# Triangular inverses of a gated delta net: 3 stream transpositions on 128 partitions per set in place of 12 on 32

## The chip, the cores and the metric

The kernel runs on one core of a Trainium2 chip. The metric is device time in microseconds (us), the median of several runs of the whole program.

## What is computed

Two layers of a diffusion backbone over 1024 latent and 256 context tokens with 1024 features. Layer 0 mixes tokens by latent attention and gated linear attention, layer 1 by a bidirectional chunked gated delta net with 8 heads; each is followed by a squared-ReLU MLP. The change touches the delta net alone. For each head, direction and chunk of 64 tokens it solves a unit lower triangular system:

```python
    a_mat = jnp.where(strict, jnp.einsum('bhnid,bhnjd->bhnij', kb, k) * decay, 0.0) + jnp.eye(C, dtype=F32)
    rhs = jnp.concatenate([v * beta, kb * jnp.exp(g)[..., None]], axis=-1)
    sol = lax.linalg.triangular_solve(a_mat, rhs, left_side=True, lower=True)
```

The kernel forms the inverse of each 64x64 matrix from its two 32x32 diagonal blocks and the product that fills the corner.

## The kernel before

TensorE runs the dense projections of layer 1 in program order: `dense1` takes a chunk of 128 output features at a time, in blocks of 512 or 256 tokens; a block of 512 is 24 matmuls (three products of split operands times eight slices of the features, lines 181 to 183) into one of four PSUM tiles `ps`. Queries and keys come first, then eight chunks of values, then the output gates. For queries, keys and values the block is emptied by ScalarE (L1146) and by two VectorE additions of the short convolution (L1151); for the gates by one SiLU on ScalarE (L1449).

All other work of this stage is in generators, called lanes. After each block, `pump` lets every lane go on by a share of the block's time, so that its instructions are written between the dense ones; each engine then runs what it has in that order. `drain` writes out what is left in the lanes once five gates have been projected. Three gates follow the drain, and then the scans of the delta net.

`inv_lane` makes the inverses in five sets, in the order 0, 1, 4, 2, 3: sets 0 to 3 are the latent chunks of a pair of heads, set 4 the context chunks of all pairs. A set is 32 matrices of 64x64 (two directions, 16 chunks) for each of the two heads of a pair; the head and the row lie on the partitions, so that each quarter of 32 partitions holds the rows of one 32x32 diagonal block. A set goes as follows.

- Products of keys, TensorE `pk` (L1349); VectorE multiplies them into `Nm` and, but for set 4, query-key products into `Am` (L1352).
- Four VectorE stream transpositions, one per quarter, bring the diagonal blocks of `Nm` into `X` (L1365).
- The loop: 30 steps of two VectorE operations on all 128 partitions (L1371 and L1373), the forward substitution of all blocks at once.
- GpSimd masks `X` (L1376) and sets its diagonal (L1377).
- Eight stream transpositions, two per quarter: one into `W` (L1386), one into `Y` (L1387). GpSimd copies a part of `W` into `Y` and clears the corner of `Y` (L1389, L1390).
- `inv_tail`, two pumps later: TensorE makes `pq` from `Nm` and `W` (L1403), ScalarE copies it to `Q` (L1407); in the next pump TensorE makes `pu` from `Q` and `W` (L1417), ScalarE copies it into the corner of `Y` (L1420), and GpSimd scales and stores `Y`.

`decay_lane` prepares the decays of the sets ahead. It has two buffers for `Nm`, and starts on a set when `state["inv"]` of the set two before it has been marked. GpSimd also makes the low parts of the weights (`wlo`, L170), ScalarE their high parts (`whi`, L167).

Of the kernel before, what the change touches and what calls it, by code (L numbers as in the profile page):

```python
# [8 lines left out]
F32 = mybir.dt.float32  # L9
# [12 lines left out]
T = LAT + CTX  # L22
# [11 lines left out]
def hybrid_backbone(ctx: ExitStack, tc: tile.TileContext, a, out, taps=None):  # L34
# [25 lines left out]
    def pump(us):  # L60
        """advances every lane: a lane yields the vector engine's time of what it emitted, or None to wait for the next call."""
        for it in list(lanes):
            gen, w = it
            t = us * w
            while t > 0:
                try:
                    d = next(gen)
                except StopIteration:
                    lanes.remove(it)
                    break  # L70
                if d is None:
                    break
                t -= d
# [39 lines left out]
    def ada_lane(l, mods, cols, wpool, accpool, ppool, ptag, wait=1):  # L113
        """modulations of layer l: products on the vector engine, sums over the partitions on the tensor engine."""
# [25 lines left out]
    def ada_first(m, half, wpool, ypool, ppool):  # L140
        """half of a modulation of layer 0 before there is other work: products on the tensor engine, then transposed."""
# [43 lines left out]
    def group(ps, n, nk, w, x, rate, every=1e9):  # L185
        """ps = sum over k of w(k)^T x(k), split operands; the lanes advance by rate of its time."""
# [12 lines left out]
    def rsqrt_small(p, ssq, n, dim, gain=1.0):  # L199
        """ssq: AP [128, n] (sums); returns tile [128, n] with gain/sqrt(mean + eps): a seed from the exponent, a step of  # L200
        third and one of second order."""
# [16 lines left out]
    def rsqrt_pool(p, ssq, n, dim):  # L218
        """as rsqrt_small, on the pool engine."""
# [13 lines left out]
    def stat_lane(hs, c0, n, tp, small, pp, ptag, dim, inc=False, engs=(V, G)):  # L233
        """1/rms of the tokens c0..c0+n over the features in the tiles hs, [128 tokens, n/128]; inc: as the tiles are made."""
# [22 lines left out]
    def spread(r, nt, pp, ptag):  # L257
        """r [128 tokens, nt] along the free dimension, the same on every partition: PSUM [128, nt * 128]."""
# [10 lines left out]
    def norm_lane(hs, c0, n, A, B, dst, tp, small, pp, ptag, r=None, inc=False, rb=None, ks=range(KD)):  # L269
        """a = rms(h) * A + B of a block of tokens, split into dst(k)."""  # L270
# [21 lines left out]
    class Act:  # L292
        """split activations [features, tokens] in tiles of one block of tokens."""
# [13 lines left out]
    # =========================================================== layer 0 mixer  # L307
# [23 lines left out]
    def gla_gates(g):  # L331
        """per head: decays of both directions (partitions 0..63 forward, 64..127 backward), decayed queries and keys."""
# [62 lines left out]
    def gla_main(g):  # L395
        """per head: states before every chunk, outputs, norm over the head, gate; transposed into d_mix."""
        f_order = list(range(16, 20)) + list(range(16))
        b_order = list(range(19, 15, -1)) + list(range(15, -1, -1))
        for h in range(4):
# [4 lines left out]
            # a chunk's outer product goes to the slot of the state after it  # L404
# [109 lines left out]
    with ExitStack() as e1:  # L514
# [146 lines left out]
        def latent(j, i, hs):  # L661
            """a chunk of the query (j = 0) or key-value (j = 1) latents, with its part of the sums of squares."""
# [26 lines left out]
    # ---- multi-head latent attention: scores transposed, minus the queries' maxima in a row of the contraction  # L689
# [7 lines left out]
    def proj(m, nm, kt, xh, xl, w, pp, tag):  # L697
        """generator of the projected blocks."""
# [8 lines left out]
    with ExitStack() as e2:  # L707
# [26 lines left out]
        # values  # L734
# [12 lines left out]
        # rotated query parts, scaled  # L747
# [54 lines left out]
    def prep0(k, b, eng):  # L802
        """a chunk of the heads' outputs, split for the output projection."""
# [5 lines left out]
    with ExitStack() as e2:  # L809
# [8 lines left out]
        def pair_ops(m):  # L818
            """projections of the heads 2m, 2m + 1 into their slots, a block of tokens at a time."""
# [24 lines left out]
        def max_ops(hd, b):  # L844
            """the row maxima of the scores of a block of queries into the contraction's last row: subtracted as rounded to
            the leading part, which the softmax does not depend on."""
# [91 lines left out]
    # =========================================================== output projection, residual; MLP  # L938
# [7 lines left out]
    def out_proj(l, wname, passes, mix, prep, base, act, add, stack, wp, w, span, sp=None):  # L946
        """h = base + gate * (mix @ w) in passes over blocks of tokens; prep[b]: what makes the blocks of pass b."""
# [42 lines left out]
    def mlp(l, blocks, tail_blocks, act, lanes_in, tail, wp, then=None):  # L990
        """h += gate * mlp(act); lanes_in(pools) makes the blocks after the first, tail(pools, b) follows a finished block."""
# [105 lines left out]
    # =========================================================== layer 1 mixer: gated delta rule  # L1097
    # A chunk of a head pair sits on the partitions as (head of the pair, token of the chunk or key feature).
    d_h = dram.tile([KD, 128, T], F32, name="d_h")
    d_X = [dram.tile([128, NC, 3, 64], F32, name=f"d_X{m}") for m in range(4)]          # keys transposed, keys, queries transposed  # L1100
# [9 lines left out]
    with ExitStack() as e1:  # L1110
# [12 lines left out]
        with ExitStack() as e2:  # L1123
# [16 lines left out]
            # ---- short convolution over tokens, SiLU  # L1140
# [25 lines left out]
            def qk_lane(y, nt, gain, m, key):  # L1166
                """a pair of conv'd heads: rows of length gain, to DRAM as they are (keys) and transposed."""
# [46 lines left out]
            # ---- gates  # L1214
# [22 lines left out]
            gx, gy = iv.tile([128, 2, 4, NC], F32, name="gx", tag="Q", bufs=2), iv.tile([128, 2, 4, NC], F32, name="gy", tag="tm")  # L1237
# [37 lines left out]
            # ---- decays, triangular inverses and masked query-key products of 32 chunks, both directions  # L1275
# [12 lines left out]
            def decay_lane():  # L1288
                """exp(-|g_i - g_j|) of a set; m < 4: the latent chunks of pair m, m == 4: the context chunks of all pairs."""
# [528 lines left out]
```

## Time and profile before

| | us |
|---|---|
| median of 3 runs (3552.53 to 3554.66) | 3552.6 |
| span of the profiled execution, first to last instruction | 3550.4 |
| TensorE busy in the span | 3322.8 (94%) |
| VectorE busy | 2329.7 (66%) |
| ScalarE busy | 1156.1 (33%) |
| GpSimd busy | 1077.5 (30%) |
| the inversions, from the first set's products to the last set's `pu` | 2106 to 2478 |

The profile gives one time for the profiled execution, its span; the 2.2 us to the median lie around it. PE is TensorE, DVE is VectorE, ACT is ScalarE, POOL is GpSimd. Busy time of an engine is the time in which an instruction of its own runs; matmuls are pipelined, so their recorded durations overlap. A wait is put down to the instruction whose end came last.

### The profile page before, as it was taken

Reading aid. Unit: us, or ns where it says so; the run is one execution under the profiler, and the core shown is the slowest. Engines: PE = TensorE matmul, PEld = TensorE weight load, DVE = VectorE, ACT = ScalarE, POOL = GpSimd, SP = SyncE. Lnnn points to the kernel's source line nnn. Section 1 sums busy time; section 2 is a strip of 40 time slices with the busy share of each in tenths; the row PEclk is TensorE's granted clock in tenths of the full one; section 3 lists DMA queues with packets and bytes.
Section 4 is the critical chain, followed back from the end, with each engine's and each line's share of the span. In section 5 each row is a group of like instructions: output and inputs, shape, how many; then the busy total and the mean of one; then the engine's idle time right before and its main releaser. Section 6 shows DMA issues by size and latency. Waiting matters only on the chain.

```text
span 3550.4 us, 47773 instructions
## 1 busy us (share of the span) xinstructions
PE 3322.8 (94%) x18372; PEld 2736.7 (77%) x18372; DVE 2329.7 (66%) x3986; ACT 1156.1 (33%) x2153; POOL 1077.5 (30%) x809
## 2 busy tenths in 40 slices
PE   8998988999989999999999997877999999999998
PEld 4876766666778888888888776666888788888887
DVE  4847556888768777776445779998466554444445
ACT  3143336555423111111211453332465421111212
POOL 3212125556642111111211332334025522222223
PEclk9988889999989999999999999998999999999999
DMA  5622224101422222221111233333664211111111
GB/s 191 216 71 64 59 92 105 26 21 50 149 88 84 75 82 80 76 82 62 45 39 36 72 101 90 90 83 103 143 131 131 72 48 48 48 48 48 48 54 60
DMA packets 279155, 285.06 MB, mean 80 GB/s; under 512 B 152176, under 2 KB 217264, under 8 KB 278928
## 3 DMA queue, kind: packets, MB, share of 16 engines
q1 hardware_dynamic: 267120, 260.78, 25.3%
q0 software_dynamic: 5760, 10.75, 1.3%
q10 hardware_dynamic: 6048, 10.49, 0.9%
q8 instruction: 144, 2.36, 0.3%
q14 instruction: 83, 0.68, 0.1%
HBM read 228.67 MB, written 53.28 MB: 79 GB/s over the span
## 4 chain that ended last, share of the span: by engine, by line
PE 71%; DVE 17%; issue 4%; ACT 3%; DMA 3%; POOL 2%; SPq 0%; DVEq 0%; ACTq 0%; POOLq 0%
PE ps L181 17%; PE ps L183 17%; PE ps L182 17%; DVE acc L126 2%; DVE tm L1371 2%; DVE gst L445 1%; DMA adaw<-in_adaw_dram 1%; DVE X L1373 1%; PE S L181 1%; DVE y L1151 1%; PE S L183 1%; PE S L182 1%; PE pa L1620 1%; DVE X L1365 1%; PE M L855 1%
## 5 line engine op out<-in xcount | busy, mean ns | idle before, releaser
L170 POOL TENSOR_TENSOR wlo<-wst,whi 128x1024 fp32r<-128x1024 f32 (+1 forms) x207 | 488.6, 2368 | 1553.1 <-ACT whi L167 1528.4
L181 PE MATMUL ps<-th,whi 128*128 128x512 f32 (+1 forms) x1304 | 480.5, 368 | 4.9 <-DVE h L1045 3.4
L183 PE MATMUL ps<-th,wlo 128*128 128x512 f32 (+1 forms) x1304 | 477.4, 366 | 2.4 <-POOL wlo L170 2.4
L167 ACT CAST whi<-wst 128x1024 fp32r<-128x1024 f32 (+2 forms) x213 | 212.6, 1012 | 820.1 <-PE ps L182 740.1
L182 PE MATMUL ps<-tl,whi 128*128 128x512 f32 (+1 forms) x1304 | 478.4, 367 | 0.0
L1010 DVE TENSOR_TENSOR rl<-rl 128x512 f32<-128x512 f32 (+1 forms) x160 | 214.5, 1341 | 346.0 <-ACT rl L1009 345.8
L181 PE MATMUL ps<-mxh,whi 128*128 128x512 f32 (+1 forms) x1008 | 356.5, 354 | 0.0
L183 PE MATMUL ps<-mxh,wlo 128*128 128x512 f32 (+1 forms) x1008 | 351.1, 349 | 1.1 <-POOL wlo L170 1.1
L182 PE MATMUL ps<-mxl,whi 128*128 128x512 f32 (+1 forms) x1008 | 351.5, 349 | 0.0
L126 DVE SCALAR_TENSOR_TENSOR acc<-adaw,sc,acc 128x256 f32<-128x256 f32 (+1 forms) x476 | 293.8, 661 | 42.5 <-DMA adaw<-in_adaw_dram 42.0
L1045 DVE SCALAR_TENSOR_TENSOR h<-ps,mod,h 128x512 f32<-128x512 f32 (+1 forms) x384 | 243.8, 657 | 96.4 <-PE ps L183 94.7
L181 PEld LDWEIGHTS ps<-th,whi 128*128 128x128 f32 x1304 | 247.4, 190 | 48.7 <-DVE h L1045 4.7
L183 PEld LDWEIGHTS ps<-th,wlo 128*128 128x128 f32 x1304 | 247.0, 189 | 43.6 <-POOL wlo L170 3.2
L182 PEld LDWEIGHTS ps<-tl,whi 128*128 128x128 f32 x1304 | 247.6, 190 | 38.9
L1045 DVE SCALAR_TENSOR_TENSOR g<-ps,mod,g 128x512 f32<-128x512 f32 (+1 forms) x264 | 188.5, 731 | 106.3 <-PE ps L183 106.1
L914 POOL TENSOR_TENSOR pl<-P,ph 128x512 fp32r<-128x512 f32 x144 | 179.7, 1262 | 114.3 <-DVE ph L913 78.9
L181 PEld LDWEIGHTS ps<-mxh,whi 128*128 128x128 f32 x1008 | 194.4, 193 | 25.8 <-issue 1.2
L182 PEld LDWEIGHTS ps<-mxl,whi 128*128 128x128 f32 x1008 | 194.4, 193 | 24.9 <-issue 1.4
L183 PEld LDWEIGHTS ps<-mxh,wlo 128*128 128x128 f32 x1008 | 194.2, 193 | 25.0 <-POOL wlo L170 1.5
L183 PE MATMUL ps<-m1h,wlo 128*128 128x512 f32 x512 | 203.9, 398 | 0.0
L181 PE MATMUL ps<-m1h,whi 128*128 128x512 f32 x512 | 203.8, 398 | 0.0
L182 PE MATMUL ps<-m1l,whi 128*128 128x512 f32 x512 | 203.6, 398 | 0.0
(373 smaller groups left out, 7011.6 us busy)
## 6 DMA issues: line engine op xcount, KB each, us to landing
wst<-in_w_dram SPq DMA_DIRECT2D x128, 512.0 KB, 3.5
adaw<-in_adaw_dram SPq DMA_DIRECT2D x224, 128.0 KB, 2.1
adaw<-in_adaw_dram SPq DMA_DIRECT2D x80, 256.0 KB, 3.6
wst<-in_owT_dram SPq DMA_DIRECT2D x25, 512.0 KB, 3.8
wst<-in_ewo_dram SPq DMA_DIRECT2D x16, 512.0 KB, 3.7
wY<-d_YA SPq DMA_DIRECT2D x64, 128.0 KB, 3.2
wst<-in_owo_dram SPq DMA_DIRECT2D x16, 512.0 KB, 3.7
wst<-in_ewT_dram SPq DMA_DIRECT2D x14, 512.0 KB, 4.6
```

Source lines behind the costliest of these rows:

```text
L126: V.scalar_tensor_tensor(out=acc[c], in0=w, scalar=sc[:, k, c:c + 1], in1=acc[c], op0=ALU.mult, op1=ALU.add)
L167: S.copy(out=hi, in_=src)
L170: lo_eng.tensor_tensor(out=lo, in0=src, in1=hi.bitcast(F32), op=ALU.subtract)
L181: PE.matmul(ps, hi_w, hi_x, start=first, stop=False)
L182: PE.matmul(ps, hi_w, lo_x, start=False, stop=False)
L183: PE.matmul(ps, lo_w, hi_x, start=False, stop=last)
L445: V.scalar_tensor_tensor(out=stt[p0:p0 + 64, c2, :], in0=stt[p0:p0 + 64, c, :], scalar=ge[p0:p0 + 64, c:c + 1], in1=stt[p0:p0 + 64, c2, :] ...
L855: PE.matmul(ps[:, :kn_], qh[0:96, qt * 128:(qt + 1) * 128], kh[0:96, k0:k0 + kn_], start=True, stop=True)
L914: (V if j % 4 == 3 else G).tensor_tensor(out=pl[:, :n], in0=P_[:, :n], in1=ph[:, :n].bitcast(F32), op=ALU.subtract)
L1010: V.tensor_tensor(out=r[:, :n], in0=r[:, :n], in1=r[:, :n], op=ALU.mult)
L1045: V.scalar_tensor_tensor(out=h[m][:, c0:c0 + n], in0=ps[:, :n], scalar=mod[l][:, 40 + m, c:c + 1], in1=h[m][:, c0:c0 + n], op0=ALU.mult, o ...
L1371: V.tensor_tensor(out=t3, in0=X[:, k + 1:, k:k + 1].to_broadcast([128, n, k]), in1=X[:, k:k + 1, :k].to_broadcast([128, n, k]), op=ALU.mult)
```

## The change

Per set, ScalarE first copies the second diagonal block of each head to the columns of the first, inside `Nm` (two copies on 32 partitions). One stream transposition on 128 partitions then makes `X` from all four quarters. After the loop two more, `U[1]` and `U[0]`, give the inverse blocks in both orientations; eight copies of 32x512, four on ScalarE and four on GpSimd, place the diagonal blocks in `Y`. `Q` no longer has a tile: it is written over the first columns of `Nm`. `inv_tail` marks `state["inv"]` one pump later, after `pu`. The lane tells `pump` less time for its transpositions: 2.0 and 2 times 2.1 in place of 4 times 1.15 and 4 times 2.3. All other lines of the difference are comments.

```diff
-            gx, gy = iv.tile([128, 2, 4, NC], F32, name="gx", tag="Q", bufs=2), iv.tile([128, 2, 4, NC], F32, name="gy", tag="tm")
+            gx, gy = iv.tile([128, 2, 4, NC], F32, name="gx"), iv.tile([128, 2, 4, NC], F32, name="gy", tag="tm")
...
-                    for q in range(4):
-                        qs, f0 = slice(32 * q, 32 * q + 32), 32 * (q % 2)
-                        V.transpose(out=X[qs], in_=Nv[qs, :, f0:f0 + 32].rearrange("p b f -> p f b"))
-                        yield 1.15
+                    for p in range(2):
+                        qs = slice(64 * p + 32, 64 * p + 64)
+                        S.copy(out=Nv[qs, :, 0:32], in_=Nv[qs, :, 32:64])
+                    V.transpose(out=X, in_=Nv[:, :, 0:32].rearrange("p b f -> p f b"))
+                    yield 2.0
...
-                    W = iv.tile([128, 32, 32], F32, name="W")
-                    Yv = Y.rearrange("p z c f -> p (z c) f")
-                    for q in range(4):
-                        qs, f0 = slice(32 * q, 32 * q + 32), 32 * (q % 2)
-                        fA = X[qs]                                   # -> U
-                        fB = X[qs].rearrange("p r c -> p c r")       # -> U^T
-                        w_in, y_in = (fB, fA) if q % 2 == 0 else (fA, fB)
-                        V.transpose(out=W[qs].rearrange("p b f -> p f b"), in_=w_in)
-                        V.transpose(out=Yv[qs, :, f0:f0 + 32].rearrange("p b f -> p f b"), in_=y_in)
-                        z = 1 if q % 2 == 0 else 0
-                        G.tensor_copy(out=Y[qs, z, :, f0:f0 + 32], in_=W[qs, 16 * z:16 * z + 16])
-                        G.memset(Y[qs, z, :, 32 - f0:64 - f0], 0.0)
-                        yield 2.3
-                    lane(inv_tail(m, Nv, W, Y), front=True)
+                    U = [iv.tile([128, 32, 32], F32, name=f"U{z}") for z in range(2)]
+                    for z, src in ((1, X.rearrange("p r c -> p c r")), (0, X)):
+                        V.transpose(out=U[z].rearrange("p b f -> p f b"), in_=src)
+                        for q in range(4):
+                            qs, f0 = slice(32 * q, 32 * q + 32), 32 * (q % 2)
+                            src = U[z][qs, 16 * z:16 * z + 16]
+                            if q % 2:
+                                S.copy(out=Y[qs, z, :, f0:f0 + 32], in_=src)
+                            else:
+                                G.tensor_copy(out=Y[qs, z, :, f0:f0 + 32], in_=src)
+                            if z != q % 2:
+                                G.memset(Y[qs, z, :, 32 - f0:64 - f0], 0.0)
+                        yield 2.1
+                    lane(inv_tail(m, Nv, U, Y), front=True)
...
-                Q = []
+                Q = [Nv[:, 16 * z:16 * z + 16, 0:32] for z in range(2)]
...
-                            PE.matmul(pq[r0 + 32:r0 + 64, b, :], Nv[r0:r0 + 32, z * 16 + b, 32:64], W[r0:r0 + 32, z * 16 + b, :],
+                            PE.matmul(pq[r0 + 32:r0 + 64, b, :], Nv[r0:r0 + 32, z * 16 + b, 32:64], U[1][r0:r0 + 32, z * 16 + b, :],
                                       start=True, stop=True, tile_position=(r0, r0 + 32))
-                    Q.append(iv.tile([128, 16, 32], F32, name="Q", bufs=2))
...
-                state["inv", m] = True
                 yield None
...
-                            Qb, Wb = Q[z][r0 + 32:r0 + 64, b, :], W[r0 + 32:r0 + 64, 16 * z + b, :]
+                            Qb, Wb = Q[z][r0 + 32:r0 + 64, b, :], U[0][r0 + 32:r0 + 64, 16 * z + b, :]
...
+                state["inv", m] = True
```

On VectorE, between the loop of the second set (1) and that of the third (4), the program of before has these rows. The name before an arrow is what an instruction writes, and the shape is partitions by elements.

```order
L1373 TENSOR_TENSOR X<-X,tm 128x30
L1386 STREAM_TRANSPOSE W<-X 32x32x32
L1387 STREAM_TRANSPOSE Y<-X 32x32x32
L1386 STREAM_TRANSPOSE W<-X 32x32x32
...
L1387 STREAM_TRANSPOSE Y<-X 32x32x32
L1151 SCALAR_TENSOR_TENSOR y<-ps,cw,y 128x255
L1352 TENSOR_TENSOR Nm<-pk,Nm 128x512
L1151 SCALAR_TENSOR_TENSOR y<-ps,cw,y 128x255
L1352 TENSOR_TENSOR Nm<-pk,Nm 128x512 x3
L1151 SCALAR_TENSOR_TENSOR y<-ps,cw,y 128x511
L1365 STREAM_TRANSPOSE X<-Nm 32x1024 x2
```

At the same place the changed program has these, up to the first step of the next loop.

```order
L1375 TENSOR_TENSOR X<-X,tm 128x30
L1310 TENSOR_TENSOR Nm<-pG,gcum 128x512 x2
L1384 STREAM_TRANSPOSE U_18930<-X 128x32x32
L1384 STREAM_TRANSPOSE U_18929<-X 128x32x32
L1151 SCALAR_TENSOR_TENSOR y<-ps,cw,y 128x255 x2
L1151 SCALAR_TENSOR_TENSOR y<-ps,cw,y 128x511 x4
L1151 SCALAR_TENSOR_TENSOR y<-ps,cw,y 128x1
L1151 SCALAR_TENSOR_TENSOR y<-edge,cw,y 128x1
L1352 TENSOR_TENSOR Nm<-pk,Nm 128x512 x4
L1151 SCALAR_TENSOR_TENSOR y<-ps,cw,y 128x255 x2
L1367 STREAM_TRANSPOSE X<-Nm 128x1024
L1373 TENSOR_TENSOR tm<-X 128x30
```

Eight transpositions have become two and four have become one, and two blocks' convolutions (the rows of 511 elements) stand between the two sets' transpositions where one stood.

On ScalarE, at the end of the stage before the drain, the program of before has these rows: the copies of `pq` and `pu` of set 2 and then of the last set, 3, among the gates' SiLU (`sg`, one per block) and the weights' casts.

```order
L1407 COPY Q<-pq 32x512 x4
L1449 ACTIVATE sg<-ps 128x512 x2
L1420 COPY Y<-pu 32x16x32 x4
L167 CAST whi<-wst 128x1024
L1449 ACTIVATE sg<-ps 128x512 x2
L167 CAST whi<-wst 128x1024
L1449 ACTIVATE sg<-ps 128x512
L1407 COPY Q<-pq 32x512 x4
L1420 COPY Y<-pu 32x16x32 x4
```

The changed program has these there, from the gather of set 3 (L1366) over its copies out of `U` (L1389) to its `pq` (the second L1409).

```order
L1366 COPY Nm<-Nm 32x32x32 x2
L1451 ACTIVATE sg<-ps 128x512
L167 CAST whi<-wst 128x1024
L1409 COPY Nm<-pq 32x16x32 x4
L1451 ACTIVATE sg<-ps 128x512 x2
L1421 COPY Y<-pu 32x16x32 x4
L167 CAST whi<-wst 128x1024
L1451 ACTIVATE sg<-ps 128x512
L1389 COPY Y<-U_20803 32x16x32 x2
...
L1451 ACTIVATE sg<-ps 128x512
L167 CAST whi<-wst 128x1024
L1451 ACTIVATE sg<-ps 128x512 x2
L167 CAST whi<-wst 128x1024
L1409 COPY Nm<-pq 32x16x32 x4
```

Seven blocks of gates now stand between the gather of the last set and its `pq`, and the copies out of `U` stand in ScalarE's order ahead of two casts of weights and of the blocks that TensorE fills meanwhile.

## Rows read from the trace of the kernel before

**Rows 1.** The page: span, and busy tenths of two engines in 40 equal slices.
```profile
span 3550.4 us, 47773 instructions
...
PE   8998988999989999999999997877999999999998
...
DVE  4847556888768777776445779998466554444445
```

**Rows 2.** Windows of the inversions: stretch, length, busy (count) of PE, PEld, DVE, ACT, POOL; PEclk; DMA.
```profile
2106.00:2277.00 171.00, 135.15 (x1159) 112.01 (x1156) 164.55 (x290) 65.58 (x108) 53.07 (x36) 0.91 0.40 95
2277.00:2446.00 169.00, 150.24 (x1638) 124.65 (x1638) 157.19 (x249) 61.76 (x93) 64.48 (x46) 0.95 0.37 99
2446.00:2478.00 32.00, 11.58 (x266) 9.33 (x265) 26.10 (x40) 5.78 (x10) 11.02 (x13) 0.56 0.12 34
```

**Rows 3.** Waits of PE, 2106 to 2478: total us, times, longest.
```profile
PE pt L1207 <- DVE Nm L1352: 23.5, 2, 14.4
PE pq L1403 <- DVE W L1386: 20.4, 2, 13.2
```

**Rows 4.** Groups of DVE instructions, 2106 to 2478: busy us, mean ns; idle before.
```profile
L1371 DVE TENSOR_TENSOR tm<-X 128x30 f32<-128x30 f32 (+9 forms) x150 | 72.7, 485 | 3.7
L1373 DVE TENSOR_TENSOR X<-X,tm 128x30 f32<-128x30 f32 (+9 forms) x150 | 63.4, 423 | 3.8
...
L1386 DVE STREAM_TRANSPOSE W<-X 32x1024 f32<-32x1024 f32 x20 | 40.5, 2024 | 14.0 <-POOL X L1377 13.5
L1387 DVE STREAM_TRANSPOSE Y<-X 32x1024 f32<-32x1024 f32 x20 | 40.3, 2017 | 0.1
L1365 DVE STREAM_TRANSPOSE X<-Nm 32x1024 f32<-32x1024 f32 x20 | 40.1, 2004 | 0.3
```

**Rows 5.** Windows of L1386 alone (three rows), then L1365 alone (one): DVE busy (count).
```profile
2106.00:2277.00 171.00, 16.12 (x8) 0.91 0.40 95
2277.00:2446.00 169.00, 16.72 (x8) 0.95 0.37 99
2446.00:2478.00 32.00, 7.63 (x4) 0.56 0.12 34
...
2277.00:2446.00 169.00, 24.06 (x12) 0.95 0.37 99
```

**Rows 6.** DVE reads of PSUM, 512 elements, on 2 and on 128 partitions.
```profile
L149 DVE COPY evt<-py x4: 671/679/679, 16.3 to 57.2; 2x512 f32<-2x512 f32 x4
...
L1307 DVE TENSOR_TENSOR Nm<-pG,gcum 128x512 f32<-128x512 f32 x12 | 8.1, 684 | 0.0
```

**Rows 7.** Timeline of DVE and POOL in the last set's loop: start, us.
```profile
2431.62 2.16 DVE L1371 TENSOR_TENSOR tm<-X 128x108 f32<-128x108 f32 x1
...
2431.72 1.92 POOL L1421 TENSOR_TENSOR Y<-Y,beta 128x1024 f32<-128x1024 f32 x1
```

**Rows 8.** Windows of the last set's loop, L1371 alone, then L1373 alone: DVE busy (count).
```profile
2430.00:2454.00 24.00, 11.84 (x30) 0.91 0.41 123
...
2430.00:2454.00 24.00, 9.97 (x30) 0.91 0.41 123
```

**Rows 9.** ACT, 2106 to 2478: its longest kind of wait on DVE; its copies of 32x512.
```profile
ACT sqn L1178 <- DVE ssq L1179: 33.5, 6, 16.4
...
L1407 ACT COPY Q<-pq 32x512 f32<-32x512 f32 x20 | 11.6, 578 | 22.6 <-PE pq L1403 22.3
```

**Rows 10.** Timeline of PE and DVE at the drain, and the window 2467 to 2480.
```profile
2435.42 0.39 PE L181 MATMUL ps<-m0h,whi 128*128 128x512 f32 x1
...
2440.86 0.39 PE L181 MATMUL ps<-mxh,whi 128*128 128x512 f32 x1
...
2467.20 3.62 PE L1403 MATMUL pq<-W,Nm 32*32 32x32 f32 x126 [7.25 <-DVE W L1386]
...
2457.68 1.91 DVE L1386 STREAM_TRANSPOSE W<-X 32x1024 f32<-32x1024 f32 x1 [3.78 <-POOL X L1377]
...
2467.00:2480.00 13.00, 12.80 (x266) 10.63 (x267) 11.13 (x15) 4.61 (x8) 6.11 (x5) 0.50 0.09 21
```

More of the change, by code (lines that the diff above doesn't have):

```diff
@@ L1378, in inv_lane, with inv_tail @@
                     Y = iv.tile([128, 2, 16, 64], F32, name="Y")
-                    W = iv.tile([128, 32, 32], F32, name="W")
-                    Yv = Y.rearrange("p z c f -> p (z c) f")
-                    for q in range(4):
-                        qs, f0 = slice(32 * q, 32 * q + 32), 32 * (q % 2)
-                        fA = X[qs]
-                        fB = X[qs].rearrange("p r c -> p c r")
-                        w_in, y_in = (fB, fA) if q % 2 == 0 else (fA, fB)
-                        V.transpose(out=W[qs].rearrange("p b f -> p f b"), in_=w_in)
-                        V.transpose(out=Yv[qs, :, f0:f0 + 32].rearrange("p b f -> p f b"), in_=y_in)
-                        z = 1 if q % 2 == 0 else 0
-                        G.tensor_copy(out=Y[qs, z, :, f0:f0 + 32], in_=W[qs, 16 * z:16 * z + 16])
-                        G.memset(Y[qs, z, :, 32 - f0:64 - f0], 0.0)
-                        yield 2.3
-                    lane(inv_tail(m, Nv, W, Y), front=True)
-            def inv_tail(m, Nv, W, Y):
+                    U = [iv.tile([128, 32, 32], F32, name=f"U{z}") for z in range(2)]
[12 more added lines that the diff above has]
+                    lane(inv_tail(m, Nv, U, Y), front=True)
+            def inv_tail(m, Nv, U, Y):
                 yield None
                 yield None
-                Q = []
+                Q = [Nv[:, 16 * z:16 * z + 16, 0:32] for z in range(2)]
                 for z in range(2):
```

## Prediction

> **What bounds the kernel now.** I read the page first. TensorE is busy for nine tenths of most slices; there is a dent in slices 25 to 28 of the 40, counted from 1, where it falls to seven or eight tenths while VectorE rises to eight or nine [rows 1]. A slice is 88.8 us, so the dent is at about 2130 to 2485 us: the inversions. I then cut this stage into three windows [rows 2]. The reader is to compare the columns of PE and DVE. From 2106 to 2277 (sets 0 and 1; call it A) VectorE works 164.6 of 171 us and TensorE 135.2, so TensorE stands still for 36. From 2277 to 2446 (B, up to the drain) it is 157.2 and 150.2 of 169, TensorE idle for 19. From 2446 to 2478 (C, the drain) TensorE works 11.6 of 32 and is idle for 20.4. That is 75 us in which TensorE, the engine that bounds the rest of the program, waits. The waits of PE name the reason [rows 3]: the longest two kinds end with a VectorE instruction, `Nm` products that hold PSUM (23.5 us) and the transposition into `W` that the last set's `pq` needs (20.4). VectorE is the bound of A, nearly that of B, and its chain is the bound of C.
>
> **What is removed and added on VectorE.** The transpositions of 32x1024 take 2.02 us in the mean, 60 of them 120.9 us [rows 4]. They become 15 of 128x1024. No row shows that form. From below it costs what 1024 elements on each of fewer partitions cost, 2.02 us; from above, if the four quarters went one after another, four times that, 8.1. The nearest rows with other widths are VectorE reads of 512 elements: 0.679 us on 2 partitions, 0.684 on 128 [rows 6]. The number of partitions does not show there, so I take 2.02: 15 cost 30.3, and VectorE is rid of 90.6 us. By window: A holds 24 (eight in each of the three lines), B 12, 8 and 8, C 4 and 4 [rows 5], L1387 as L1386. So A gives 18 x 2.02 = 36.4, B 21 x 2.02 = 42.4, C 6 x 2.02 = 12.1.
>
> The Trainium skill ("VectorE: DVE Perf Modes", The three transpose paths) has VectorE transposing 128x128 in bf16 as a 4x4 grid of 32x32 blocks in 311 ns. No run here shows it; an estimate from it, all quarters side by side, would leave the sum as it is.
>
> **What gets dearer on VectorE.** The steps of the loop are stretched now and then: one of 108 elements lasted 2.16 us, and ended with a GpSimd operation on 1024 elements that ran beside it [rows 7]. The last set's loop was busy for 11.84 + 9.97 = 21.8 us, of which that one collision is 1.9, so a clean loop is 19.9 [rows 8]. Five loops took 72.7 + 63.4 = 136.1 [rows 4]; 136.1 - 5 x 19.9 = 36.6 us are collisions. The transpositions keep their 2.0 us in all three lines. GpSimd's work stays about the same while VectorE's 348 us (sum of the three windows) become 257; if collisions grow as the room shrinks, they rise by 36.6 x (348 / 257 - 1) = 13 us, of which I put 6 in A and 7 in B. The bounds are 0 and, if each of the 90.6 us had been as exposed as a loop step (36.6 / 136.1), 24.
>
> The Trainium skill ("SBUF — State Buffer", Who interferes with whom) says that a VectorE instruction with two SBUF inputs contends with a GpSimd instruction that reads SBUF, and one with a single input does not. By that rule the transpositions were time in which GpSimd ran for nothing, and this speaks against the change; the trace agrees as far as the 2.16 us go. By the rule gone wrong, with no contention, the sum below would be some 6 us better.
>
> **What is added on ScalarE and GpSimd.** A 32x512 copy on ScalarE takes 0.58 us [rows 9]. Per set there are four such copies, and two of 32x1024, which I bound by twice that, 1.16 each: 4.6 us per set, 23 in all. ScalarE is busy for 133 of 372 us [rows 2], so its time is covered. Its order is not free: the gather must end before `X` is transposed, 2.3 us per set. In four sets the `Am` products, four VectorE operations, stand between; for set 4 I count 2. GpSimd makes as many copies and clears as before. The later mark of `state["inv"]` delays only the decays of a set two further on, by one block; I count nothing, since each set's decays are to be ready while a loop of over 20 us runs.
>
> **The sum.** A: VectorE's work is 164.6 - 36.4 + 6 = 134 us; with the 6.4 in which it stood still before, 141. TensorE's 135 is now as large. Two engines so evenly loaded that wait on each other in order do not fit into the larger of the two; I add 4, about a tenth of the 36 lost now. A: 171 to 145, a gain of 26.
>
> B: VectorE 157.2 - 42.4 + 7 + 2 = 124 against TensorE's 150. TensorE is the bound, and most of its 19 us of idle time goes; I keep 4. B: 169 to 154, a gain of 15.
>
> C: the question is whether VectorE has reached `U[1]` of the last set when TensorE reaches its `pq`. By the order on ScalarE shown above, seven blocks of gates lie between the gather and that `pq`. A block lasts 2440.86 - 2435.42 = 5.44 us [rows 10], seven 38. VectorE needs, from the gather: 2.3, `X` 2.0, the loop 24 the length of its window [rows 8], 3.8 for GpSimd's mask [rows 10], `U[1]` 2.0, together 34. It fits with 4 us to spare, so the 20.4 us go. TensorE's clock was granted at 0.50 from 2467 to 2480 after that wait, 1.2 GHz [rows 10]; of these 13 us half would not be needed, and I take 5, hence a gain of 25 for C, less the 5 that I give it for a late start of the loop: 20.
>
> Together 26 + 15 + 20 = 61 us. The span of 3550.4 becomes 3489.4; with the 2.2 us to the median as before, 3552.6 becomes **3491.6 us**. What follows the drain is not on VectorE: three gates of 10.9 us each, and then the scans, whose first loads have that time as before.
>
> **The rivals.** *ScalarE blocks.* ScalarE runs in order, and the copies out of `U` make it wait for VectorE; behind them stand blocks to be emptied, and casts of weights that TensorE needs. Before, it waited like that on VectorE 6 times for 33.5 us, 16.4 at the most [rows 9]. For: the copies stand ahead of two casts in the order shown above. Against: TensorE has four `ps` tiles, 4 x 5.44 = 22 us, before it must stop, and the old waits were longer than what VectorE will be late. If each of the five sets lost 6 us of TensorE by it, 30 us come back: 3522.
>
> *All idle time goes.* If VectorE is no longer late anywhere, TensorE gets back its 75 us and about 10 of slow clock (0.91, 0.95 and 0.56 in the three windows): 3552.6 - 85 = 3467. Against it: A stays evenly loaded.
>
> *The transposition is paid by quarter.* At 8.1 us each the 15 cost what the 60 did; the gathers then stand bare on VectorE's path (5 x 2.3 = 11.5), of which perhaps half shows: slower, 3558. From about 7.8 us each, where 15 x 7.8 and 5 x 0.8 of gather equal the 120.9, nothing is gained. Only rows 6 speak against it, and a transposition is no plain read.
>
> *It does not matter.* If TensorE's idle time were kept by the order of the lanes, and not by VectorE's work, the time would stay within 7 us of 3552.6. Against: VectorE is at 96% in A.
>
> **How the numbers follow.** Forecast 62 in 100 (its own range 3476 to 3508: the 24 us of collisions and no stall in A and B, either way), ScalarE blocks 17, all idle goes 12, paid by quarter 5, does not matter 4. To hold 8 in 10, the range reaches to the larger part of the first two rivals: 3470 to 3522. A difference of 0.2%, 7 us, is about what these runs can tell from none. The forecast and the first two rivals are faster; I leave a little room for mixtures: faster 0.88, same 0.05, slower 0.07.
>
> **What would show it.** Right: 15 transpositions of 128x1024 at about 2.0 us; VectorE's busy time in the stage down by 75 to 90; TensorE idle for under 20 us from the first `pk` to the last `pu`, and the wait of `pq` on VectorE gone at the drain; the first scan 55 to 65 us earlier. The loop's means up from 485 and 423 ns would show the collisions. Wrong: transpositions near 8 us; waits of TensorE that end with a ScalarE cast or emptying, ScalarE itself waiting on `U`; or TensorE's 20 us at the drain still there.

## The result, and the profile after

| | median us | runs | range | ratio to before, 95% |
|---|---|---|---|---|
| before | 3553.6 | 4 | 3552.5 to 3561.5 | |
| changed | 3506.9 | 4 | 3498.2 to 3518.5 | 0.9863, 0.984 to 0.9886 |
| changed, second time (before beside it 3557.2) | 3502.9 | 5 | 3501.5 to 3515.8 | 0.9856, 0.9833 to 0.9879 |
| changed, third time (before beside it 3550.2) | 3505.3 | 5 | 3501.6 to 3515.0 | 0.9871, 0.9849 to 0.9894 |

The change makes the kernel faster by 47, 54 and 45 us against the kernel before of the same batch. The forecast was 61 us less, 3491.6; the first time lies in the stated range, 15 us above the forecast.

The page of the changed kernel's first profile: span, and the busy tenths of TensorE and VectorE in 40 equal slices.

```profile
span 3516.8 us, 47746 instructions
...
PE   7998898999989999999999998999999999999998
...
DVE  4837556888877877777544668885565544444445
```

Beside [rows 1]: of the dent in TensorE's slices 25 to 28 one slice of eight tenths is left, and VectorE has there 8, 8, 8 and 5 tenths instead of 9, 9, 9 and 8. This execution is the slowest of its four. It is late before it reaches the changed code: its first `pG`, the decays' first product, starts at 2071.2 us, in the kernel before at 2056.9, after the same program. Over the profiles of this study, with that part unchanged in all of them, this moment lies between 2053.9 and 2073.0. So I compare stretches, from the same matmul to the same matmul, and not spans.

The next view is windows, with the columns of [rows 2]: length, busy time of PE, PEld, DVE, ACT, POOL, granted clock. I cut the stage where TensorE has done the same work as at the ends of A, B and C before: 461 dense matmuls (L181 to L183) in A, 546 in B, the rest up to the last `pu` in C. First the first profile of the changed kernel, below it the third.

```profile
2119.80:2279.40 159.60, 140.65 (x1430) 117.19 (x1430) 139.02 (x304) 81.89 (x130) 52.74 (x36) 0.93 0.42 102
2279.40:2430.50 151.10, 144.15 (x1382) 120.02 (x1381) 118.12 (x221) 69.20 (x102) 73.01 (x57) 0.99 0.42 110
2430.50:2437.00 6.50, 6.50 (x264) 5.33 (x263) 0.00 (x0) 5.43 (x9) 2.40 (x2) 1.00 0.17 69
```

```profile
2107.90:2263.40 155.50, 139.34 (x1431) 115.92 (x1431) 137.40 (x304) 81.93 (x130) 52.66 (x37) 0.95 0.44 106
2263.40:2414.40 151.00, 144.09 (x1383) 119.94 (x1381) 117.91 (x221) 69.18 (x102) 72.43 (x57) 0.99 0.42 110
2414.40:2420.80 6.40, 6.40 (x264) 5.27 (x263) 0.00 (x0) 5.37 (x9) 2.35 (x1) 1.00 0.17 66
```

A is 160 or 156 us long where it was 171, B 151 where it was 169, C 6.5 where it was 32 [rows 2]. VectorE's busy time in the three together is 257.1 (139.0 + 118.1) against 347.8, 90.7 us less. TensorE stands still for 19 us in A, 7 in B and none in C; in the third profile it is 16, 7 and none. The counts of PE, 1430 and 1382 against 1159 and 1638 [rows 2], show that some small matmuls have moved: the `pq` and `pu` of set 1, 256 in all, lie in A now and lay in B before. In C TensorE works at the full clock, 1.00, where it had 0.56.

The groups of VectorE in the changed stage, with busy time and mean duration, answer to [rows 4].

```profile
L1375 DVE TENSOR_TENSOR X<-X,tm 128x30 f32<-128x30 f32 (+9 forms) x150 | 66.1, 440 | 4.0
L1373 DVE TENSOR_TENSOR tm<-X 128x30 f32<-128x30 f32 (+9 forms) x150 | 64.5, 430 | 4.0
...
L1384 DVE STREAM_TRANSPOSE U<-X 128x1024 f32<-128x1024 f32 x10 | 20.6, 2127 | 8.0 <-POOL X L1379 8.0
...
L1367 DVE STREAM_TRANSPOSE X<-Nm 128x1024 f32<-128x1024 f32 x5 | 10.1, 2021 | 2.9 <-ACT Nm L1366 2.9
```

The 15 transpositions of 128x1024 are busy for 30.7 us: four times the partitions cost about what 32 did. The two lines of the loop together take 130.6 us, against 136.1 [rows 4].

TensorE's waits in the changed stage and up to the scans answer to [rows 3].

```profile
PE pa L1605 <- ACT sg L1451: 7.0, 1, 7.0
PE pt L1175 <- DVE Nm L1352: 6.6, 1, 6.6
PE pt L1207 <- DVE Nm L1307: 4.5, 2, 2.8
PE pG L1304 <- ACT sqn L1178: 4.3, 1, 4.3
PE pt L1207 <- ACT edge L1148: 4.1, 1, 4.1
```

The wait of `pq` on the last set is gone, and so are the two of `pt` (L1207) on the products `Nm` (L1352), 23.5 us. Other waits of `pt` on `Nm` are there: one of 6.6 us in A (L1175) and two in B, 4.5 together. The first line is new, and lies behind the stage: the first scan, two matmuls after its start, waits for a ScalarE instruction of the last gate.

What holds that instruction is read from SyncE's queue in the same profile: start, us from the first to the last issue of the row, line, transfer and count.

```profile
2424.42 11.03 SPq L1452 DMA_DIRECT2D d_g<-sg  x2
2440.09 6.29 SPq L1497 DMA_DIRECT2D wY<-d_YA  x8
2446.42 3.36 SPq L1485 DMA_DIRECT2D wX<-d_X  x4
...
2468.30 1.04 SPq L1486 DMA_DIRECT2D wv<-d_v  x1
2469.43 0.85 SPq L1452 DMA_DIRECT2D d_g<-sg  x2
```

And the end of the chain of waits up to the scans:

```profile
2434.51 0.61 ACT sg L1451
2435.13 4.49 DMA d_g<-sg
...
2440.09 0.62 SPq L1497
...
2469.43 5.63 DMA d_g<-sg
2475.17 0.61 ACT sg L1451
2475.82 1.71 PE pa L1605 x6
```

To be read so: the store of the gates projected before the drain ends at 2439.6; VectorE clears `wY` only then (it waits 19.5 us for that store), and the first loads of the scans start at 2440.1; 38 loads are issued one by one in the next 29 us; the store of the next gates stands behind them and is issued at 2469.4; only when it has landed does ScalarE write the last gate's block, and the scan's matmul waits for that.

In the kernel before the same store was issued at 2502.6, 8 us ahead of the first scan matmul at 2510.4. There the first loads of `wY` began at 2450.6, 60 us ahead of the scan; here they lead it by 28 (2440.1 to 2468.4). Of the missing 32 us 25 are the shorter C. Most of the rest lies ahead of the store: ScalarE copies `pq` four times before it empties the block, and the store takes 4.5 us. In the kernel before ScalarE emptied this block ahead of the copies of `pq`, and the store ran beside the stop:

```profile
2447.27 0.59 ACT L1449 ACTIVATE sg<-ps 128x512 f32<-128x512 f32 x1
2469.15 1.18 ACT L1407 COPY Q<-pq 32x512 f32<-32x512 f32 x2 [21.29 <-PE pq L1403]
```

### The profile page after: what moved, and what is told of

Read it like the earlier page. It is cut to its first block, busy times and chain, and to the rows that moved or that the text cites. A ratio compares the mean times of both kernels' runs of the same rounds, so it can differ in the third digit from the quotient of the medians.

```text
span 3516.8 us, 47746 instructions
## 1 busy us (share of the span) xinstructions
PE 3326.5 (95%) x18372; PEld 2738.1 (78%) x18372; DVE 2237.3 (64%) x3941; ACT 1180.6 (34%) x2183; POOL 1079.1 (31%) x809
## 4 chain that ended last, share of the span: by engine, by line
PE 70%; DVE 16%; ACT 4%; issue 4%; DMA 3%; POOL 2%; SPq 1%; DVEq 0%; ACTq 0%; POOLq 0%
PE ps L181 17%; PE ps L182 17%; PE ps L183 17%; DVE acc L126 2%; DVE gst L445 2%; DMA adaw<-in_adaw_dram 1%; DVE X L1375 1%; DVE tm L1373 1%; PE S L181 1%; PE S L183 1%; PE S L182 1%; PE pa L1622 1%; PE pa L1594 1%; PE M L855 1%; PE acc L875 1%
## 5 line engine op out<-in xcount | busy, mean ns | idle before, releaser
L181 PE MATMUL ps<-th,whi 128*128 128x512 f32 (+1 forms) x1304 | 479.7, 368 | 6.7 <-DVE h L1045 5.0
L183 PE MATMUL ps<-th,wlo 128*128 128x512 f32 (+1 forms) x1304 | 476.5, 365 | 2.4 <-POOL wlo L170 2.4
L181 PE MATMUL ps<-mxh,whi 128*128 128x512 f32 (+1 forms) x1008 | 355.9, 354 | 0.0
L183 PE MATMUL ps<-mxh,wlo 128*128 128x512 f32 (+1 forms) x1008 | 350.6, 348 | 0.7 <-POOL wlo L170 0.5
L181 PEld LDWEIGHTS ps<-th,whi 128*128 128x128 f32 x1304 | 246.7, 189 | 50.9 <-DVE h L1045 7.1
L183 PEld LDWEIGHTS ps<-th,wlo 128*128 128x128 f32 x1304 | 246.4, 189 | 43.5 <-POOL wlo L170 3.3
L181 PEld LDWEIGHTS ps<-mxh,whi 128*128 128x128 f32 x1008 | 193.9, 193 | 25.8 <-issue 1.2
L183 PEld LDWEIGHTS ps<-mxh,wlo 128*128 128x128 f32 x1008 | 193.6, 192 | 24.8 <-POOL wlo L170 1.5
L183 PE MATMUL ps<-m1h,wlo 128*128 128x512 f32 x512 | 204.0, 398 | 0.0
L181 PE MATMUL ps<-m1h,whi 128*128 128x512 f32 x512 | 203.8, 398 | 0.0
```

The lines of the kernel that those rows point to most:

```text
L181: PE.matmul(ps, hi_w, hi_x, start=first, stop=False)
L183: PE.matmul(ps, lo_w, hi_x, start=False, stop=last)
```

## The experiments

### Four times each transposition

```diff
-                    V.transpose(out=X, in_=Nv[:, :, 0:32].rearrange("p b f -> p f b"))
+                    for _ in range(4):
+                        V.transpose(out=X, in_=Nv[:, :, 0:32].rearrange("p b f -> p f b"))
...
-                        V.transpose(out=U[z].rearrange("p b f -> p f b"), in_=src)
+                        for _ in range(4):
+                            V.transpose(out=U[z].rearrange("p b f -> p f b"), in_=src)
```

> The changed kernel with each of its 15 transpositions on 128 partitions issued four times in a row, so that VectorE works as long on transpositions as before (60 times 2.0 us), while the order of the lanes, the copies and everything else stay as changed. If the gain is VectorE's time (theory), the stage from the first decay matmul to the first scan matmul goes from 408 us back to 445 to 460 us (456 before) and the time to 3540 to 3560 us. If the gain is the other order and pace of the lanes (rival), it stays within 10 us of 408 and 3507 us.

Measured: 3566.5 us, 1.0036 of before (1.002 to 1.0052). Its three windows, cut as above, and VectorE's groups:

```profile
2112.40:2288.20 175.80, 142.49 (x1431) 117.84 (x1431) 164.03 (x292) 81.44 (x130) 52.21 (x36) 0.91 0.40 94
2288.20:2467.00 178.80, 151.46 (x1382) 126.16 (x1381) 170.75 (x267) 66.11 (x97) 65.26 (x46) 0.92 0.36 94
2467.00:2492.60 25.60, 10.19 (x263) 8.36 (x262) 14.88 (x11) 8.70 (x14) 11.15 (x13) 0.56 0.06 22
```

```profile
L1386 DVE STREAM_TRANSPOSE U<-X 128x1024 f32<-128x1024 f32 x40 | 75.7, 2024 | 7.3 <-POOL X L1380 7.3
L1376 DVE TENSOR_TENSOR X<-X,tm 128x30 f32<-128x30 f32 (+9 forms) x150 | 75.6, 504 | 3.5
L1374 DVE TENSOR_TENSOR tm<-X 128x30 f32<-128x30 f32 (+9 forms) x150 | 74.6, 497 | 3.5
```

With VectorE's busy time back at 349.7 us, the stops are back in all three windows, the one at the drain with its clock of 0.56, and the whole gain is gone. The rest of the change (two copies per set for the gather, half of the copies on ScalarE, the later mark) does not help by itself: with it, and with VectorE's time given back, the kernel is 11 us slower than before. The gain is VectorE's time.

One thing does not come back with the stop: the lead of the scans' loads. The last block ahead of the drain is emptied at 2489.0, behind the copies out of `U` and of `pq` that the stop holds up; the first load of `wY` is issued at 2493.3, 1.2 us after the last `pu`, and the first scan waits 4.3 us for the last gate.

### The lane's times as before

```diff
-                    yield 2.0
+                    yield 4.6
...
-                        yield 2.1
+                        yield 4.6
```

> The changed kernel, but its lane declares the old times to the pump (4.6 for the first transposition and twice 4.6 for the other two). Theory (VectorE's time): within 12 us of the changed kernel, 3500 to 3520 us; some of the wait of the last set's product at the drain may come back, since the lane ends later against the dense blocks. Rival (pace): at least half of the 47 us is lost, 3530 us or more.

Measured: 3511.6 us, 0.9875 (0.985 to 0.99).

### The new times in the kernel before

```diff
-                        yield 1.15
+                        yield 0.5
...
-                        yield 2.3
+                        yield 1.05
```

> The kernel before, whose lane declares the times of the change to the pump (2.0 in all for the transpositions before the loop, 4.2 for those after it) and keeps its twelve transpositions on 32 partitions. Theory (VectorE's time): within 10 us of the kernel before, 3545 to 3565 us, since VectorE has as much to do. Rival (pace): at least half of the 47 us is gained, 3530 us or less.

Measured: 3566.8 us, 1.0033 (1.0016 to 1.0049). The two together: the pace at which `pump` writes the lane out is not the cause. The changed kernel keeps its gain, within the intervals, with the old times, and the new times alone make the kernel before slower by 10 us.

In the profile of the kernel before with the new times the drain has no stop any more, since the lane's work is written earlier. But TensorE stands still for 78 us from the first `pG` to the last `pu`, as before (77): the stops lie in A and B. And it waits at the first scan:

```profile
PE pt L1207 <- DVE Nm L1352: 31.9, 2, 20.0
PE ps L181 <- DVE rs_t L214: 16.0, 1, 16.0
...
PE pa L1603 <- ACT sg L1449: 7.0, 1, 7.0
```

So the pace moves VectorE's lateness to another place; it does not remove it.

### The gather alone

The transpositions after the loop are those of before; only `X` is made by two copies and one transposition.

```diff
-                    for q in range(4):
-                        V.transpose(out=X[qs], in_=Nv[qs, :, f0:f0 + 32].rearrange("p b f -> p f b"))
+                    for p in range(2):
+                        S.copy(out=Nv[qs, :, 0:32], in_=Nv[qs, :, 32:64])
+                    V.transpose(out=X, in_=Nv[:, :, 0:32].rearrange("p b f -> p f b"))
```

> The kernel before with only the first part of the change: the two gathering copies on ScalarE and one transposition on 128 partitions in place of four; the eight transpositions after the loop stay. Theory: 15 of the 45 transpositions that the change removes are gone, 30 us of VectorE's time, so about a third of the gain, 12 to 20 us: 3533 to 3542 us. Rival (ScalarE's gather blocks): no gain or slower, 3550 us or more.

Measured: 3531.9 us, 0.9931 (0.9909 to 0.9954), 23 less than before and 1 below what was expected. Its windows:

```profile
2110.90:2273.90 163.00, 142.71 (x1302) 117.74 (x1302) 155.40 (x290) 73.89 (x117) 51.82 (x36) 0.92 0.41 101
2273.90:2447.10 173.20, 155.04 (x1511) 127.08 (x1509) 155.71 (x263) 63.97 (x95) 68.21 (x54) 0.93 0.35 97
2447.10:2453.50 6.40, 6.40 (x264) 5.28 (x263) 4.92 (x3) 5.33 (x9) 4.53 (x5) 1.00 0.18 67
```

### The part after the loop alone

The four transpositions into `X` are those of before; `U` is as changed.

```diff
-                    for p in range(2):
-                        S.copy(out=Nv[qs, :, 0:32], in_=Nv[qs, :, 32:64])
-                    V.transpose(out=X, in_=Nv[:, :, 0:32].rearrange("p b f -> p f b"))
+                    for q in range(4):
+                        V.transpose(out=X[qs], in_=Nv[qs, :, f0:f0 + 32].rearrange("p b f -> p f b"))
```

> The changed kernel with the four transpositions on 32 partitions before the loop put back and no gather; the two on 128 partitions after the loop stay. Theory: 30 of the 45 transpositions are gone, 60 us of VectorE's time, so about two thirds of the gain, 27 to 40 us: 3513 to 3527 us, and with the gather alone it adds up to the whole change. Rival (the copies out of U on ScalarE block): under 15 us, 3538 us or more.

Measured: 3513.4 us, 0.9884 (0.9863 to 0.9905), 42 less than before.

```profile
2103.10:2263.30 160.20, 142.44 (x1430) 118.85 (x1430) 151.09 (x296) 75.40 (x124) 52.69 (x37) 0.91 0.42 101
2263.30:2425.90 162.60, 147.65 (x1382) 121.68 (x1381) 140.56 (x244) 64.82 (x98) 72.09 (x57) 0.96 0.39 101
2425.90:2432.40 6.50, 6.50 (x264) 5.34 (x263) 0.00 (x0) 5.43 (x9) 2.82 (x3) 1.00 0.26 100
```

The two halves gain 23 + 42 = 65 us, the whole 45 to 54, so they do not add up to it, as had been expected. The third window says why: either half alone makes VectorE early enough at the drain, and C falls from 32 us to 6.5 in both. A gain that both halves make counts once. In A and B together, 340 us before, the gather gives 4, the part after the loop 17 and the whole 29 to 34, more than their sum.

### One transposition fewer

The second transposition after the loop is left out and its places are filled from the first; the matmuls and copies stay.

```diff
-                    U = [iv.tile([128, 32, 32], F32, name=f"U{z}") for z in range(2)]
+                    U = [iv.tile([128, 32, 32], F32, name="U1")] * 2
...
-                        V.transpose(out=U[z].rearrange("p b f -> p f b"), in_=src)
+                        if z:
+                            V.transpose(out=U[z].rearrange("p b f -> p f b"), in_=src)
```

> The changed kernel without the second transposition: the one U serves both places, so that half of the inverses are transposed wrongly, and VectorE has 5 x 2.1 = 10.5 us less to do. If VectorE is still the bound of the inversions: 8 to 10 us less than the change. If TensorE and VectorE are evenly loaded there and wait on each other in turn, so that each further us saved on VectorE is worth about a third (34 us saved gave 12): 2 to 5 us less. If TensorE alone is the bound: nothing.

Measured: 3502.5 us, 0.9853 (0.9831 to 0.9876), beside 3505.3 for the change.

```profile
2104.20:2260.20 156.00, 139.70 (x1430) 116.60 (x1430) 135.53 (x302) 81.52 (x130) 52.79 (x37) 0.93 0.44 106
2260.20:2409.60 149.40, 143.90 (x1382) 119.98 (x1381) 112.01 (x218) 69.14 (x102) 72.93 (x57) 0.99 0.43 111
```

VectorE works 247.5 us in the two windows instead of 255.3 in the third profile of the change, and the windows are as long as there, within 2 us. So VectorE's amount of work no longer bounds B, where 6 of these 8 us lie; 2.8 us of difference in the medians does not tell a third of the saving from none of it. TensorE still stands idle for 16 us in A; but only 2 us of the saving lie there, so for A by itself this run says little.

### All copies out of `U` on GpSimd, twice

```diff
-                            if q % 2:
-                                S.copy(out=Y[qs, z, :, f0:f0 + 32], in_=src)
-                            else:
-                                G.tensor_copy(out=Y[qs, z, :, f0:f0 + 32], in_=src)
+                            G.tensor_copy(out=Y[qs, z, :, f0:f0 + 32], in_=src)
```

> The changed kernel with all eight copies out of U per set on GpSimd, so that ScalarE no longer waits for the transpositions after the loop (it waited 9.3 us for them and 9.0 for the store of the tile Y). If ScalarE's order costs TensorE something (theory of the rival in the prediction), 3 to 10 us faster than the changed kernel; if not, within 3 us, or slower by GpSimd's later low parts of the weights.

> All eight copies out of U on GpSimd, again. If ScalarE's waits on U (9.3 us) and on a store of Y (9.0) cost TensorE time in the changed kernel: 5 to 9 us less than the change in this batch, and an idle time of TensorE from the first pG to the first scan near 30 us against 35 to 37. If they cost nothing: within 3 us of the change.

Measured: 3495.9 us, 0.9833 (0.981 to 0.9856), beside 3502.9 for the change, and 3498.4 us, 0.9845 (0.9825 to 0.9866), beside 3505.3. Both times the median is 6.9 us lower; the intervals of the ratios overlap. What these copies do to ScalarE in the changed kernel stands in its groups, busy time and mean behind the first bar, idle time before them behind the second:

```profile
L1389 ACT COPY Y<-U 32x512 f32<-32x512 f32 x20 | 12.4, 618 | 18.5 <-DVE U L1384 9.3 <-DMA d_YA<-Y 9.0
...
L1366 ACT COPY Nm<-Nm 32x1024 f32<-32x1024 f32 x10 | 10.5, 1045 | 11.6 <-DVE Nm L1352 9.0 <-DVE rs_s L206 2.5
```

Without the first group, A of the second of these runs is this long, and B 150.6:

```profile
2100.10:2254.20 154.10, 139.19 (x1430) 116.12 (x1430) 138.00 (x304) 76.94 (x122) 57.47 (x45) 0.93 0.44 107
```

In the first it was 152.8; the change's A was 159.6, 158.7 and 155.5 in its three profiles. One wait makes most of this difference: `pt` on ScalarE's `edge`, 4.1 us in the first two profiles of the change, 0.9 in the third, and absent with the copies on GpSimd. But the second sign set for the second run does not hold: TensorE's idle time from the first `pG` to the first scan is 30 and 31 us with the copies on GpSimd, and 35, 37 and 32 in the change, so the third profile has it without the edit. And of the 11 us between the spans of the second batch's two profiled executions 8 lie ahead of the first `pG`. That ScalarE's 18.5 us of waiting ahead of these copies cost TensorE some us is made likely by the medians of two batches, not settled.

### The last gates' stores issued from GpSimd

```diff
-            def gates(r, p, tag, rate):
+            def gates(r, p, tag, rate, q=nc.sync):
...
-                    nc.sync.dma_start(out=d_g1[hh], in_=sg[:, :LAT])
+                    q.dma_start(out=d_g1[hh], in_=sg[:, :LAT])
...
-            gates(range(8 - LATE, 8), ev, "sg", 0.0)
+            gates(range(8 - LATE, 8), ev, "sg", 0.0, G)
```

> The changed kernel with the stores of the last three gates (those after the drain) issued from GpSimd and not behind the scans' loads in SyncE's queue. If the 7 us for which TensorE stands still at the first scan matmuls come from that queue (theory: the third gate's last SiLU waits for a buffer that such a store frees), they go, and the time falls by 5 to 8 us against the changed kernel run beside it. If TensorE waits for the loads themselves (rival), the 7 us stay and the time is within 3 us of it.

Measured: 3502.6 us, 0.9845 (0.9823 to 0.9868), beside 3502.9 for the change. TensorE's waits from the drain on:

```profile
PE pa L1622 <- ACT vk L1609: 2.0, 4, 0.9
PE pb L1643 <- ACT O L1614: 1.3, 2, 0.9
...
PE pa L1605 <- ACT sg L1451: 0.2, 1, 0.2
```

The wait is gone, and the time is the same. So neither theory holds as it was put. Counted from the last `pu`, these scan matmuls (`pa` and `pb` together) start after so many us:

| | first | ninth | 101st | 301st |
|---|---|---|---|---|
| before | 33.5 | 34.9 | 47.1 | 73.3 |
| change, second profile | 32.2 | 42.1 | 55.8 | 81.7 |
| last stores from GpSimd | 32.2 | 33.6 | 47.7 | 79.5 |
| both edits (below) | 32.2 | 33.6 | 47.4 | 78.6 |

Eight of the 8.5 us won at the ninth matmul stand at the 101st, 2.2 at the 301st. In between the chains wait on each other's results in short pieces. That they wait for loads that are still late is likely, since the loads start no earlier than in the change (`wY` 3.8 us after the last `pu`), but the waits name ScalarE and VectorE, all but one of 0.5 us on `wY`, and I could not settle it. Loads that start earlier were not tried.

### Both edits

All copies out of `U` on GpSimd, and the last gates' stores issued there.

> The changed kernel with two edits together: all eight copies out of U on GpSimd, and the last gates' stores issued from GpSimd. In the profiles the first alone shortened the inversions by 7 us (TensorE idle 37 to 30), the second alone took the 7.9 us wait before the first scan away but gave some 6 of it back within the next 300 scan matmuls. If both act by themselves: 9 us less than the change in this batch, 0.981 of before. If the copies' 7 us are chance: 2 us less than the change. If GpSimd, now with more to do, is late with the last set's stores: no better than the change.

Measured: 3497.0 us, 0.9837 (0.9815 to 0.986), beside 3505.3 for the change and 3498.4 for the copies alone. It is the lowest of its batch, 8 us below the change and 1 below the copies alone; the second edit adds nothing that can be measured.

### The change again

> The changed kernel again, beside the others: 3500 to 3512 us, with the stage up to the last small product some 55 us shorter than before, and the 7 us at the first scan matmuls in its profile again.

> The changed kernel a third time, beside the three others: 0.986 of before, 3500 to 3510 us.

Measured: the second and third rows of the first table's changed kernel. From the first `pG` to the last `pu` the three profiles of the change take 365.2, 362.7 and 358.5 us, before 420.3. The kernel before has one profile, so that its side of these differences is one execution.

## Why the prediction was right, and where its sizes were off

**The bound and the mechanism: right.** The stops of TensorE were VectorE's lateness, in A partly by way of ScalarE (below). Giving the time back brings them back; neither the pace nor the rest of the edit makes the gain.

**The transposition's price: right.** 15 x 2.02 = 30.3 us were forecast, 30.7 came, and VectorE's work fell by 90.7 where 90.6 less collisions had been taken. The rival by which each quarter is paid is refuted. The Trainium skill ("VectorE: DVE Perf Modes", The three transpose paths) gives 311 ns for 128x128 in bf16; eight times that, an estimate from the page, is 2.5 us for 128x1024, and the fp32 form measured 2.02 to 2.13 in the mean. At 2.5 the 15 would have cost 7 us more than at 2.02: the prediction's remark that the page's figure leaves the sum as it is was not worked out.

**Collisions, +13: wrong in sign.** The loop's lines lost 5.5 us, though GpSimd works the same 128 us in both stages and VectorE's room had shrunk. Counted from the records, GpSimd ran beside steps of the loop for 53.7 us before, 43.6 in the first profile of the change and 67.0 with four times the transpositions; the two lines took 136.1, 130.6 and 150.2. So the loop does get dearer with the time in which GpSimd runs beside it, but this time did not grow as VectorE's work shrank. What sets it is likely the order of the instructions; no run tests that. The Trainium skill ("SBUF — State Buffer", Who interferes with whom) has an instruction of VectorE with one SBUF input, outside the two-port modes, not contend with GpSimd. The trace agrees for the transpositions: of those before, 19 had a GpSimd operation beside them for over 1 us and took 1.87 to 2.25 us, 2.06 in the mean, and 28 had none and took 2.01. But that free time did not pass to the loop when the transpositions went.

**A, from 171 to 145: too good.** It became 160, 159 and 156 us. A part is work: with the small products of set 1 in A, TensorE's 135 us became 141, 139 and 139, where the sum had kept 135; VectorE's 139, 139 and 137 stand against 134. The larger part is idle time: the 4 us for two engines that wait on each other in order were 16 to 20. The prediction put TensorE's stops in A down to VectorE by the 23.5 us on `Nm`; but only 9.1 of these lie in A. Most of the stops there ended with ScalarE:

```profile
PE pk L1349 <- ACT sqn L1178: 11.2, 1, 11.2
PE pG L1304 <- ACT sqn L1178: 6.8, 1, 6.8
PE pt L1207 <- ACT edge L1148: 5.9, 1, 5.9
```

ScalarE's `sqn` itself waited 33.5 us for VectorE [rows 9], 14.3 in the change, so a part of these stops went as well. What is left in A are single waits: in the first profile 6.6 us of `pt` on `Nm`, 4.3 of `pG` on `sqn`, 4.1 of `pt` on `edge`. With one transposition fewer the first is 4.9, with the copies on GpSimd the last is absent; so both engines' lateness has a share, and no run separates the two in A. Taking 2 us more from VectorE did not change A's length beyond its spread. This is the mildest form of the rival that ScalarE blocks: forecast at 30 us for the whole, worth about 7 by the medians, if that is no chance.

**B, 169 to 154, and C, 32 to 12: both better than that.** 151 and 6.5. B's TensorE had 6 us less to do than the sum gave it (144 against 150), mainly the products that A took over. The chain from the gather to `U[1]` did fit into the seven blocks, and the clock at the drain was whole. The 5 us kept for a late start were not needed.

Over the stage the errors nearly cancel: A, B and C lost 55, 56 and 59 us in the three profiles, 61 were forecast.

**"whose first loads have that time as before": the step that failed.** The loads of the scans start when the gates' block before the drain has been stored, and before the change they had the 20 us of the stop beside the three gates. With the stop gone they have the gates alone. Wherever a profile has no stop at the drain and SyncE issues the last gates' stores, the first scan waits for the last gate: 7.0, 7.9 and 7.0 us in the change, 7.7 and 7.4 with either half of it, 5.1 with the old times, 7.0 in the kernel before with the new ones. But a stop is a lead only if the block's emptying and store come ahead of it: with four times the transpositions the stop is there, the emptying stands behind it, and 4.3 us of the wait are there too.

The scan's ninth matmul comes 6 to 7 us later after the last `pu` than before (41.1 to 42.1 against 34.9), the 301st 8. From the first `pG` to the last `pu` the change had won 55 to 62 us; 47 to 54 of them remain, and the medians show 45 to 54. Which wait carries the 8 us past the ninth matmul stays open: with the last stores issued from GpSimd the wait is gone and 6 of the 8 us are still lost. In the first profile of the change TensorE's clock was granted at half, 1.2 GHz, from within the wait of 7.0 us to 5.8 us past its end at 2475.8:

```profile
2471.40:2481.60 10.20, 5.78 (x27) 5.78 (x28) 2.57 (x8) 2.58 (x7) 0.00 (x0) 0.50 1.03 279
```

**The other signs.** TensorE was to be idle for less than 20 us from the first `pk` to the last `pu`: 26 in the first profile, 27 in the second, 23 in the third (312.9 - 289.8). The first scan was to come 55 to 65 us earlier: counted from the first `pG`, 56 in the first profile, 63 in the third. The loop's means were to rise: they moved both ways, 485 to 430 and 423 to 440.

## What to carry to other kernels

A stop that is taken away may have been somebody's lead: before its whole length is counted as gain, list the transfers and stores that ran during it and ask who will wait for them. When two edits each remove the same stop, their gains do not add; cut the stage at equal work on the bounding engine and see in which window each one gains. And where a saving brings one engine's work down to that of another, do not take a tenth of the idle time before for their waits on each other, as was done here: in A half of it stayed, 16 to 20 us of 36. Look up in which window each wait lies, and which engine ends it.

## What the runs showed that was not expected

A stream transposition of 1024 fp32 elements per partition takes 2.02 us in the mean on 32 partitions and 2.02 to 2.13 on 128, with the strided views of this kernel.

A wait of only 7 us at the first scan was followed by 5.8 us of work at half the clock, where the 20.4 us of waiting at the drain before were followed by 13 [rows 10].

The same program, up to the same matmul, took 2053.9 to 2073.0 us in the profiles of this study. That is wider than several of the effects here, and as wide as the spread between executions of one kernel.
